# Stores of an attention-score kernel issued in turn by SyncE and ScalarE

## The chip, the cores and the metric

The kernel runs on one core of a Trainium2 chip. The metric is the time of one execution on the device, in microseconds (us), the median over several runs. Below, TensorE is PE, VectorE is DVE, ScalarE is ACT, GpSimd is POOL and SyncE is SP, as the profile names them. The DMA engines are a sixth party: the profile counts 16 of them for the core, and their queues moved 83.89 MB between HBM and the on-chip buffer SBUF. A "ring" here is what the profile lists as the DMA queue of one issuing engine. SyncE's is q1, which holds all 83.89 MB of the kernel before. ScalarE's is q10. A descriptor is one DMA record of the trace: 5120 of the 5504 in q1 before are of 16 KB, the other 384 of 4 bytes. The trace has 16 landings for each transfer, 384 for the 24 transfers; a transfer counts as landed with the last of its 16.

## The reference

For each of 8 x 8 pairs of batch and head, the product of queries and transposed keys, scaled:

```python
def setup_inputs():
    batch, heads, seq, dim = 8, 8, 512, 64
    ...   # q and k, float32, random
def reference(q, k):
    scale = 1.0 / np.sqrt(q.shape[-1])
    return (np.einsum('bhqd,bhkd->bhqk', q, k) * scale).astype(np.float32)
```

The inputs are 16.8 MB and the output 67.1 MB, so writing is four fifths of the traffic.

## The kernel before

The work is cut into four units of two batches. Each has four output tiles of 4 MB (`o`: 128 partitions of 32 KB). All loads and all output tiles share one pool, `big`, of three buffers. Loads are cast by GpSimd, transposed on TensorE, multiplied, and the results are evicted (copied from PSUM, where TensorE writes, to the output tile in SBUF) by ScalarE and VectorE in turn, eight evictions for a tile. When the eighth is done, the tile is stored by one DMA of SyncE.

```python
    big_pool = ctx.enter_context(tc.tile_pool(name="big", bufs=3))
    ...
    def evacuate(dst, src):
        nonlocal n_evac
        if n_evac % 2 == 0:
            pinned(nc.scalar.mul(out=dst, in_=src, mul=scale))
        else:
            pinned(nc.vector.tensor_scalar(out=dst, in0=src, scalar1=scale, ...))
        n_evac += 1
    ...
    def load_and_cast(v):
        xf = big_pool.tile([P, 2, 2, J * D], f32, name="big")
        ...
            nc.sync.dma_start(out=xf[:, x], in_=src[v].rearrange("p (s c) -> p s c", s=2))
        ...
    def scores(v, t):
        kT, qz = ts[v]
        o = big_pool.tile([P, 2, RO, S], f32, name="big")
        for x in range(2):
            for i in range(0, RO, 2):
                ...   # two matmuls into ps
                evacuate(o[:, x, i:i + 2, :], ps)
                yield
        nc.sync.dma_start(out=out_r[v, t], in_=o.rearrange("p x i k -> p x (i k)"))
    ...
    cast = [load_and_cast(v) for v in range(UNITS)]
    ...
    for v in range(UNITS):
        ahead = transpose(v + 1, *cast[v + 1]) if v + 1 < UNITS else iter(())
        for t in range(TILES):
            for n, _ in enumerate(scores(v, t)):
                take(ahead, 1 if v == 0 else int(n in (0, 2, 3, 5, 6)))
```

`pinned` keeps an instruction at its place in the order of its engine.

## Time and profile before

| | before |
|---|---|
| time, median of 3 runs | 202.59 us (202.53 to 202.62) |
| span of the profiled run | 200.7 us |
| VectorE, TensorE, ScalarE busy | 53%, 52%, 42% |
| DMA packets, share of 16 engines | 98.3% in one queue |
| rate over the span | 418 GB/s |

The share of busy time tells which party has no room: here only the DMA engines, at 98.3%. A wait in another engine's row then tells what that engine is held up by. It isn't in itself a cost: after the change the evictions wait 25.5 us longer for TensorE, and the time is the same. The prediction below shows the lines and reads them.

### The profile page before, as it was taken

To read this page: it belongs to the slowest core of one execution; us is meant where nothing else is said; L and a number is where in the kernel's file an instruction comes from. 1 tells how busy PE (TensorE), PEld (TensorE's weight loads), DVE (VectorE), ACT (ScalarE), POOL (GpSimd) and SP (SyncE) were. 2 spreads that over 40 slices of the span, in tenths; PEclk is the share of its full clock that TensorE was granted. 3 is DMA by queue.
4 is the path that set the end of the run, shared out by engine and by line. 5 is a ranking of instruction groups with operands and counts; after the bars stand their busy time and mean duration, and the time that the engine had idled before them with its cause. 6 is when DMAs were issued, how large, how long until landed. Compare 5 with 4: busy or idle time off the path is not lost.

```text
span 200.7 us, 1143 instructions
## 1 busy us (share of the span) xinstructions
PE 105.3 (52%) x384; PEld 45.8 (23%) x384; DVE 106.8 (53%) x98; ACT 85.0 (42%) x97; POOL 39.5 (20%) x22
## 2 busy tenths in 40 slices
PE   0035758566657465478637496748585667510000
PEld 0034535223214131224313122312121111100000
DVE  6705538486475976485749357844444444630000
ACT  2004423864755629253844384366435243620000
POOL 1299999995000000000000000000000000000000
PEclk9999576999699999957999759975858858975555
DMA  6999999999999999999999999999999999999994
GB/s 206 424 444 437 421 421 441 434 395 421 434 424 441 428 431 431 433 426 434 431 428 424 434 441 424 431 431 434 424 431 434 431 424 431 428 437 428 428 428 199
DMA packets 5509, 83.95 MB, mean 418 GB/s; under 512 B 384, under 2 KB 384, under 8 KB 384
## 3 DMA queue, kind: packets, MB, share of 16 engines
q1 hardware_dynamic: 5504, 83.89, 98.3%
q8 instruction: 3, 0.05, 0.1%
q14 instruction: 2, 0.02, 0.0%
HBM read 16.78 MB, written 67.11 MB: 418 GB/s over the span
## 4 chain that ended last, share of the span: by engine, by line
DMA 40%; DVE 10%; PE 8%; ACT 6%; issue 1%; ACTq 0%; SPq 0%; DVEq 0%
DMA out_dram<-big 40%; DVE big L68 9%; PE ps L141 8%; ACT big L66 5%; ACT qz L103 1%; DVE qz L103 1%; ACTq L66 0%; SPq L146 0%; DVEq L68 0%
## 5 line engine op out<-in xcount | busy, mean ns | idle before, releaser
L141 PE MATMUL ps<-kT,qz 128*128 128x512 bf16 x256 | 87.6, 447 | 55.5 <-ACT big L66 41.6
L68 DVE TENSOR_SCALAR big<-ps 128x1024 f32<-128x1024 f32 x64 | 78.4, 1224 | 59.8 <-PE ps L141 37.2
L66 ACT ACTIVATE big<-ps 128x1024 f32<-128x1024 f32 x64 | 65.5, 1023 | 73.0 <-PE ps L141 37.2
L141 PEld LDWEIGHTS <-qz 128*128 128x128 bf16 x256 | 27.2, 106 | 111.0 <-issue 97.5
L89 POOL CAST xb<-big 128x2048 bf16<-128x2048 f32 x16 | 38.8, 2468 | 7.9 <-DMA big<-in_k_dram 7.3
L117 PE MATMUL tp<-identity,xb 128*128 128x128 f32 x64 | 11.6, 346 | 13.4 <-POOL xb L89 13.4
L103 ACT COPY kT<-tp 64x512 f32<-64x512 f32 x16 | 9.2, 577 | 15.3 <-PE tp L117 15.1
L103 DVE COPY kT<-tp 64x512 f32<-64x512 f32 x16 | 11.0, 686 | 6.3 <-PE tp L117 6.0
L117 PEld LDWEIGHTS tp<-identity,xb 128*128 128x128 f32 x64 | 10.5, 184 | 15.2 <-POOL xb L89 13.4
L103 DVE COPY qz<-tp 64x512 f32<-64x512 f32 x16 | 11.0, 687 | 2.7 <-PE tp L125 2.5
L103 ACT COPY qz<-tp 64x512 f32<-64x512 f32 x16 | 9.6, 602 | 2.9 <-PE tp L125 2.7
L125 PE MATMUL tp<-identity,xb 128*128 128x128 f32 x64 | 9.4, 300 | 2.5 <-ACT kT L103 2.5
L125 PEld LDWEIGHTS tp<-identity,xb 128*128 128x128 f32 x64 | 8.5, 156 | 4.3 <-issue 3.3
L156 DVE MEMSET qz<- 128x4096 uint32 x2 | 6.9, 3472 | 2.5 <-PEq L184 1.7
L103 ACT ACT_TABLE_LOAD x1 | 1.3, 1283 | 0.7 <-PEq L184 0.7
masks.py:199 POOL TENSOR_SCALAR_AFFINE_SELECT identity<-identity 128x128 f32<-128x128 f32 x1 | 0.3, 292 | 0.1
masks.py:197 POOL MEMSET identity<- 128x128 f32 x1 | 0.2, 204 | 0.3 <-POOLq L184 0.3
L184 POOL MEMSET const-float32-0.0<- 128x1 f32 x1 | 0.1, 98 | 0.2 <-issue 0.2
L184 POOL MEMSET const-bfloat16-1.0<- 128x1 bf16 x1 | 0.1, 101 | 0.0
L184 POOL MEMSET const-uint8-127<- 128x1 uint8 x1 | 0.1, 101 | 0.0
L184 POOL MEMSET const-float32-1.0<- 128x1 f32 x1 | 0.1, 98 | 0.0
## 6 DMA issues: line engine op xcount, KB each, us to landing
out_dram<-big SPq DMA_DIRECT2D x16, 4096.0 KB, 20.7
big<-in_k_dram SPq DMA_DIRECT2D x4, 2048.0 KB, 18.1
big<-in_q_dram SPq DMA_DIRECT2D x4, 2048.0 KB, 22.7
```

The lines of the kernel that those rows point to most:

```text
L66: pinned(nc.scalar.mul(out=dst, in_=src, mul=scale))
L68: pinned(nc.vector.tensor_scalar(out=dst, in0=src, scalar1=scale, scalar2=None, op0=mybir.AluOpType.mult))
L89: pinned(nc.gpsimd.tensor_copy(out=xb[:, :, s].rearrange("p (g i) d e -> p g e i d", i=wide), in_=xf[:, x, s].rearrange("p (g e i d) -> p ...
L103: pinned(copy(out=dst(s, h), in_=src[:, h]))
L117: pinned(nc.tensor.transpose(out=tp[:, j, :], identity=identity, in_=kb[:, j0 + j]))
L125: pinned(nc.tensor.transpose(out=tp[:, i, jj, :], identity=identity, in_=qb[:, RO * jj + i0 + i]))
L141: pinned(nc.tensor.matmul(out=ps[:, w, :], lhsT=qz[:, i + w, n, :], rhs=kT[:, n].rearrange("d m s j -> d (m s j)"), start=True, stop=True))
L156: nc.vector.memset(qz, 0.0)
L184: nc = _bacc.Bacc("TRN2", target_bir_lowering=False, num_devices=1)
```

## The change

The intent is to let two rings hold queued stores, so that stores can come from two issuers.

```diff
-        nc.sync.dma_start(out=out_r[v, t], in_=o.rearrange("p x i k -> p x (i k)"))
+        queue = (nc.sync, nc.scalar)[t % 2]
+        pinned(queue.dma_start(out=out_r[v, t], in_=o.rearrange("p x i k -> p x (i k)")))
```

## The prediction

The "0 to 0.3 us" for uneven interleaving was the author's guess. So was it that the slowest DMA engine is one that carries the fetch, since the records carry no engine. "That time" is SyncE's time to issue a store, 0.37 us; what follows it is from the trace of before. That the heads of two rings share the engines was an assumption when it was written; how far they do is measured below (96% of the steps change the ring in the run with halves, 27% in the changed kernel).

> **What bounds the kernel now.** I read the page of the profile first, from the top, because the change concerns transfers only and the first question is whether transfers bind.
>
> ```profile
> span 200.7 us, 1143 instructions
> PE 105.3 (52%) x384; PEld 45.8 (23%) x384; DVE 106.8 (53%) x98; ACT 85.0 (42%) x97; POOL 39.5 (20%) x22
> ...
> DMA  6999999999999999999999999999999999999994
> GB/s 206 424 444 437 421 421 441 434 395 421 434 424 441 428 431 431 433 426 434 431 428 424 434 441 424 431 431 434 424 431 434 431 424 431 428 437 428 428 428 199
> ...
> q1 hardware_dynamic: 5504, 83.89, 98.3%
> ...
> HBM read 16.78 MB, written 67.11 MB: 418 GB/s over the span
> ```
>
> No compute engine is busy more than 53%. The row of DMA digits is 9 from the second slice to the last but one, and one queue alone kept the 16 DMA engines occupied for 98.3% of the span. A queue that always has a descriptor ready cannot be made readier by a second queue. I then asked whether these engines are really moving at their pace or only being held by waits. The table by stretch says the first:
>
> ```profile
> core 0: us, PE busy (x) PEld busy (x) DVE busy (x) ACT busy (x) POOL busy (x), PEclk, DMA share, GB/s
> ...
> 92.00:121.00 29.00, 19.13 (x77) 8.29 (x77) 17.18 (x16) 16.78 (x20) 0.00 (x0) 0.87 1.00 429
> 121.00:150.00 29.00, 19.40 (x60) 6.39 (x59) 17.53 (x17) 14.57 (x16) 0.00 (x0) 0.77 1.01 432
> 150.00:178.00 28.00, 16.46 (x46) 4.86 (x44) 14.68 (x12) 12.28 (x12) 0.00 (x0) 0.80 1.01 430
> 178.00:190.00 12.00, 0.00 (x0) 0.00 (x0) 0.02 (x1) 0.00 (x0) 0.00 (x0) 0.50 1.00 427
> ```
>
> The rate is 427 to 432 GB/s with compute beside it and without it (the last row, where all engines but the DMA are done). In the trace's single DMA records the transfer is 5120 descriptors of 16 KB; in every 10 us between 50 and 190 us the median of one is 0.611 us, that is 16384 / 0.611 = 26.8 GB/s for one engine and 429 for 16.
>
> Third, the waits, to see which way round the dependence goes:
>
> ```profile
> ACT big L66 <- DMA out_dram<-big: 31.3, 12, 3.5
> DVE big L68 <- DMA out_dram<-big: 15.5, 9, 2.5
> ```
>
> The evictions wait for stores to land, because the pool "big" has three buffers of 4 MB. Compute is throttled by the stores, not the reverse. Last, the queue's own view and the issue table:
>
> ```profile
> SPq L146 <- DVE big L68: 152.5, 16, 17.6
> ```
>
> ```profile
> out_dram<-big SPq DMA_DIRECT2D x16, 4096.0 KB, 20.7
> ```
>
> SyncE does wait 152.5 us for evictions, and the intent of the change may have come from a line like this. It costs nothing: a store takes 20.7 us from issue to landing while successive stores land some 9.74 us apart ((199.92 - 53.87) / 15, from the landings of the first and the last store in the trace). So about two stores are always with the engines: one moving, one queued behind it in the same ring. What the change wants to create exists already.
>
> [...] Here that time is 0.37 us for a store, 16 x 0.37 = 6 us on an otherwise empty SyncE, never in the way. [...] at 48.42 us a 16 KB instruction fetch of another queue gets in between the stores' descriptors of one engine. It also shows a price: the fetch took 0.961 us and the store's descriptor after it 0.975, both some 0.36 above 0.611. [...]
>
> **The change part by part.**
> - Bytes: unchanged, 83.89 MB, 320 descriptors of 16 KB for each DMA engine. 320 x 0.611 = 195.5 us. The first data starts at 1.75 us; the sum is 197.3. The slowest DMA engine also carries the fetch (0.96 + 0.36 = 1.3 us), which makes 198.6, and some of the turn from loads to stores near 40.5 us, where descriptors took up to 1.24 us; the last data in the trace ends at 199.5, the last landing is at 199.9. None of these terms is removed.
> - SyncE loses 8 issues, worth 8 x 0.37 = 3.0 us of a queue that idles. Gain 0.
> - ScalarE gains 8 issues. The order of instructions shows each placed after ScalarE's last eviction of a tile, waiting for VectorE's last one. At the final tile ScalarE's eviction ended at 176.98 and the store was issued at 178.09, so ScalarE would stand 1.1 us and then, if it costs there what it costs on SyncE, 0.37 us: 1.5 us, 8 times, 12 us on an engine with 85 of 200.7 us busy and 31.3 us of waits for stores before its evictions. Most falls into that wait.
> - What moves: the overlap of stores. Let W = 9.74 us be a store alone and F = 8.4 us the time to fill a tile once its buffer is free (issue minus the landing three stores earlier, or the issue before if later; 7.3 to 9.1 us over the stores from 64 us on). In one ring, when a store's data ends, two whole ones remain, 2W = 19.5 us of work. The landing is noticed about 1.6 us later (my choice: the slowest engine's lag of 1.5 us plus a little), the fill takes 8.4, so 10.0 us later, at the next issue, 9.5 us of work remain. Check: 9.5 + 9.74 + 1.5 = 20.7, the measured issue-to-landing. In two rings the two heads share the engines. When a store ends, the one behind it in its ring is whole and the one in the other ring is half done, so 1.5 W = 14.6 us remain, and at the next issue 4.6 us. The lead halves but stays positive: the DMA would run dry only if a fill took 8.4 + 4.6 = 13.0 us, against 9.1 as the longest. Adding the whole 0.4 us of the issue on ScalarE to F still leaves 4.2.
> - The residence of a store does not change: three buffers turn once in 3W = 29.2 us, of which F = 8.4 is filling, so 20.8 remain for issue to landing.
> - The start: loads keep SyncE's ring and are through at 43.0 us; the first ScalarE store would come at about 47.5 us, so no load is delayed. The end: the last two stores share the engines and finish with the total work, as before.
>
> Sum: 0 removed from the path, 0 to 0.3 us added by uneven interleaving. The time is 202.59 + 0.1 = 202.7 us (the span plus the same 1.9 us as now).
>
> **The rivals.**
> - Changing rings has a price. If each of the 256 store descriptors of a DMA engine lost the 0.36 us seen beside the fetch, 92 us would be added; a loss of 0.016 us each already makes 4 us, 2%. For it: the two lengthened descriptors. Against it: [...] the turn from loads to stores in one ring lengthened descriptors likewise, so I take the direction, not the ring, as the cause. Here both rings only write. I give it 8%, mostly as a small loss: 204 to 215 us.
> - The rings run dry. Stores that land together would free two buffers at once and leave one store with 9.7 us of work against a fill of 8.4. That is tight, and each tile that needs more than 9.7 would lose the difference, perhaps 0.5 us. Against it: one stream of compute fills tiles one after another, which puts the stagger back. 1 us in all, 203.6 us.
> - Two rings hide gaps between descriptors or stores. The table of stretches shows a DMA share of 1.00 to 1.01, so there are no gaps to hide[...].
> - A lucky placement of the fetch or of the slow engine: up to 1.3 us gained, 201.3 us.
>
> **Range and chances.** 201.4 to 204.8 us: below, the slow engine's lag gone; above, a ring dry now and then or a switch that costs 0.008 us. Faster by over 2% would need 198.5 us, less than the 198.6 of the sum above: 0.02. Slower by over 2% (206.7 us) is the price of switching: 0.07. Within 2%: 0.91.
>
> **What would show it.** Two hardware queue rows in place of one, with ScalarE's about 33.6 MB and a total share near 98%; 427 to 432 GB/s in every stretch after 64 us; a median issue-to-landing near 20.8 us on both queues; eight issues on ScalarE of some 0.4 us; evictions still waiting for stores, in total much as now. Descriptors of more than 0.63 us in the median would prove me wrong on switching, slices of DMA below 9 in the middle on dry rings[...].

## The result, and the profile after

The changed kernel takes 202.53 us (median of 4 runs, 202.52 to 202.61). The kernel before took 202.56 us in the same rounds (4 runs). The ratio is 1.0001, with a 95% interval of 0.9983 to 1.0018. A ratio here and below is the mean time of one kernel's runs over that of the other's runs of the same rounds, so it isn't quite the ratio of the medians quoted. Executions over 1.5% slower than the fastest of the same kernel are left out of the means.

From the page of the changed kernel: first span and busy shares, then the DMA share and rate in 40 slices, then queues with packets, MB and share of 16 engines.

```profile
span 200.7 us, 1129 instructions
PE 108.2 (54%) x384; PEld 47.1 (23%) x384; DVE 106.8 (53%) x98; ACT 85.0 (42%) x97; POOL 39.5 (20%) x22
...
DMA  6999999999999999999999999999999999999994
...
q1 hardware_dynamic: 3328, 50.33, 59.3%
q10 hardware_dynamic: 2176, 33.55, 39.1%
```

The DMA digits are the same 40 characters as before. The two queues together hold the DMA engines for 59.3 + 39.1 = 98.4% of the span, where one held them for 98.3%. Half of the written bytes did move to ScalarE's queue, and nothing was gained by it because there was no idle time to fill (a DMA share of 1.00 to 1.01 in the stretches before).

The same stretches as shown of before (time, busy time of each engine with counts, granted clock, DMA share, GB/s):

```profile
92.00:121.00 29.00, 19.15 (x72) 7.99 (x72) 18.23 (x19) 16.22 (x20) 0.00 (x0) 0.82 1.00 428
121.00:150.00 29.00, 17.25 (x60) 6.76 (x60) 16.82 (x16) 13.99 (x16) 0.00 (x0) 0.79 1.01 431
150.00:178.00 28.00, 17.77 (x47) 5.30 (x46) 13.47 (x11) 12.01 (x12) 0.00 (x0) 0.74 1.00 427
178.00:190.00 12.00, 4.05 (x9) 0.87 (x7) 3.67 (x3) 2.31 (x3) 0.00 (x0) 0.64 1.02 434
```

The rate is 427 to 434 GB/s, before 427 to 432. In the last row compute still runs, where before it had ended: the last store was issued at 184.0 us and not at 178.1. Its last data still landed at 199.92 us, the very same time as before. So compute got 6 us later without any cost.

The waits of engines (engine and line, waited for, total us, times, longest us); in the issue table below, the last column is the median us from issue to landing:

```profile
DVE big L68 <- PE ps L141: 51.8, 46, 4.7
ACT big L66 <- PE ps L141: 48.1, 46, 3.8
...
ACT big L66 <- DMA out_dram<-big: 19.4, 6, 4.6
...
ACT big L66 <- DVE big L68: 5.2, 3, 2.2
...
DVE big L68 <- DMA out_dram<-big: 5.0, 2, 3.4
```

Before, the first two of these were:

```profile
DVE big L68 <- PE ps L141: 37.2, 40, 1.8
ACT big L66 <- PE ps L141: 37.2, 41, 3.4
```

SyncE's own wait, and the issue table:

```profile
SPq L147 <- DVE big L68: 149.5, 8, 21.7
```

```profile
out_dram<-big SPq DMA_DIRECT2D x8, 4096.0 KB, 19.3
out_dram<-big ACTq DMA_DIRECT2D x8, 4096.0 KB, 18.0
```

Three things moved. The evictions' waits for stores fell from 31.3 + 15.5 = 46.8 us to 24.4 us. Their waits for TensorE grew from 74.4 to 99.9 us, so most of the idle time only changed its name. And ScalarE has a new wait of 5.2 us for VectorE: it stands at its DMA instruction until VectorE's last eviction is done, at one store from 64.95 us until VectorE ends at 66.64, with the issue at 66.72.

I worked some more numbers out of the single DMA records of the traces, in which each descriptor has a start and a duration. The work left at an issue is the number of descriptors issued and not yet ended, times 0.611 us, over 16 engines. The fill is counted as in the prediction. The lag is the last of a transfer's 16 landings minus their median; the median stands for the end of the store's data.

| from the fifth store on (fill and next store: from the fourth) | before | after |
|---|---|---|
| work left in the rings at an issue | 8.8 to 10.9 us | 4.0 to 7.4 us |
| work left of the next store when a store's data ends | 9.7 to 10.0 us | 6.6 to 9.7 us, mean 8.3 |
| fill of a tile, mean | 8.2 us | 8.9 us (longest 10.6) |
| median duration of a 16 KB descriptor | 0.611 us | 0.611 us |
| lag of the slowest DMA engine, apart from the last store | 1.3 to 1.7 us | 2.4 to 3.3 us |

The lead of the queue nearly halved (mean 9.9 to 5.7 us), as forecast, and was never used up. The last row I had not forecast.

### The profile page after: what moved, and what is told of

Same layout as the page of the kernel before. It is cut to its first block, busy times and chain, and to the rows that moved or that the text cites. A ratio compares the mean times of both kernels' runs of the same rounds, so it can differ in the third digit from the quotient of the medians.

```text
span 200.7 us, 1129 instructions
## 1 busy us (share of the span) xinstructions
PE 108.2 (54%) x384; PEld 47.1 (23%) x384; DVE 106.8 (53%) x98; ACT 85.0 (42%) x97; POOL 39.5 (20%) x22
## 3 DMA queue, kind: packets, MB, share of 16 engines
q1 hardware_dynamic: 3328, 50.33, 59.3%
q10 hardware_dynamic: 2176, 33.55, 39.1%
## 4 chain that ended last, share of the span: by engine, by line
DMA 30%; PE 16%; DVE 14%; ACT 7%; issue 1%; DVEq 0%; SPq 0%; ACTq 0%
DMA out_dram<-big 30%; PE ps L141 15%; DVE big L68 14%; ACT big L66 6%; ACT qz L103 1%; PE tp L117 1%; DVEq L68 0%; SPq L147 0%; ACTq L66 0%
## 5 line engine op out<-in xcount | busy, mean ns | idle before, releaser
L141 PE MATMUL ps<-kT,qz 128*128 128x512 bf16 x256 | 89.6, 465 | 58.4 <-DVE big L68 31.5
L141 PEld LDWEIGHTS <-qz 128*128 128x128 bf16 x256 | 28.0, 110 | 115.4 <-issue 102.5
L117 PE MATMUL tp<-identity,xb 128*128 128x128 f32 x64 | 10.8, 329 | 13.6 <-POOL xb L89 13.6
L103 ACT COPY kT<-tp 64x512 f32<-64x512 f32 x16 | 9.2, 577 | 15.5 <-PE tp L117 15.3
L125 PE MATMUL tp<-identity,xb 128*128 128x128 f32 x64 | 10.7, 329 | 2.5 <-ACT kT L103 2.5
## 6 DMA issues: line engine op xcount, KB each, us to landing
out_dram<-big SPq DMA_DIRECT2D x8, 4096.0 KB, 19.3
```

Source lines behind the costliest of these rows:

```text
L103: pinned(copy(out=dst(s, h), in_=src[:, h]))
L117: pinned(nc.tensor.transpose(out=tp[:, j, :], identity=identity, in_=kb[:, j0 + j]))
L125: pinned(nc.tensor.transpose(out=tp[:, i, jj, :], identity=identity, in_=qb[:, RO * jj + i0 + i]))
L141: pinned(nc.tensor.matmul(out=ps[:, w, :], lhsT=qz[:, i + w, n, :], rhs=kT[:, n].rearrange("d m s j -> d (m s j)"), start=True, stop=True))
```

## The experiments

Theory: the DMA engines set the pace with 83.9 MB at 0.611 us for 16 KB, and the number of rings and the issuing engine only change the order. The rivals were: (A) two rings did gain something and ScalarE's new work took it back, (B) changes of ring have a price, (C) a second ring hides the start of stores, (D) the halved lead costs something.

Twelve kernels ran. "Half" kernels are wrong. All seven others gave correct results.

### One ring, all stores from ScalarE

```diff
-        queue = (nc.sync, nc.scalar)[t % 2]
+        queue = nc.scalar
```

> All 16 stores are issued by ScalarE, so there is one ring again, but ScalarE carries 16 issues of 0.38 us and the waits for VectorE ahead of them. Theory (the DMA engines set the pace, and the issuing engine does not matter): 202.6 us, within 0.5 us of the kernel before; the work left in the ring at an issue is near 9.9 us as before and not near 5.5 us as after, and the slowest DMA engine lands about 1.5 us behind the median one. Rival A (two rings gave something that the cost on ScalarE took back): the cost is now doubled and the gain gone, so slower than before by the cost of 16 issues, 6 us or more, 208 us. Rival B (changing rings has a small price): a little faster than after.

Measured: 202.75 us (4 runs), the kernel before 202.48 in the same rounds, ratio 1.0009 (0.9994 to 1.0024). Sixteen issues on ScalarE in place of none moved the median by 0.3 us, so rival A, which asked for 6 us or more, falls. The lag was 1.0 to 1.8 us, that of one ring. The work left at an issue was not near 9.9 us all along. It was 2.7 to 5.3 us from 59 to 96 us and grew to about 10 us by 140 us. The third store was issued at 59.4 us, before at 56.6, and the lead had to build up again.

### Each store in two halves, one for each ring

```diff
-        queue = (nc.sync, nc.scalar)[t % 2]
-        pinned(queue.dma_start(out=out_r[v, t], in_=o.rearrange(...)))
+        rows = o.rearrange("p x i k -> p x (i k)")
+        for x, queue in enumerate((nc.sync, nc.scalar)):
+            pinned(queue.dma_start(out=out_r[v, t][:, x], in_=rows[:, x]))
```

> Every store is cut in two halves of 2 MB, one for each ring, issued together. Both rings then always work on the same tile, so that tiles land one after another as in one ring, while the DMA engines change rings all the time. Theory: 202.6 us, within 0.5 us of before; descriptors stay at 0.611 us in the median though the rings now alternate for nearly all of the stores; tiles are about 20 us from issue to landing; the slowest DMA engine's lag is back at about 1.5 us, where it was 3.1 us with stores of different tiles in the two rings. Rival B (a change of rings costs time, but in the changed kernel the rings overlapped too little to show it): with 256 changes for each DMA engine even 0.02 us each adds 5 us, 207 us.

Measured: 203.42 us (4 runs), ratio 1.0040 (1.0025 to 1.0055). My 0.5 us was missed: this is 0.9 us slower, and clear of noise. The design also wasn't what I had written. SyncE issues the first half as soon as that head is evicted, 4 to 5 us before the other half. The records do show the two rings alternating descriptor by descriptor for most of the run. When they are joined into one sequence for each engine, as described under the late loads below, 96% of the steps from one descriptor to the next between 92 and 121 us change the ring. In the changed kernel only 27% do (64 to 180 us), so that kernel alone says little about the price of a change. The median stayed at 0.611 us, so the 5 us of rival B didn't come. The lag was up to 3.3 us, not 1.5. The stretch from 92 to 121 us:

```profile
92.00:121.00 29.00, 19.04 (x73) 7.86 (x72) 18.33 (x18) 15.94 (x20) 0.00 (x0) 0.85 1.01 431
```

With rings changing all the time, 431 GB/s, within the 427 to 432 of the kernel before.

### Halves in the last three quarters only

```diff
+        if v == 0:
+            pinned(nc.sync.dma_start(out=out_r[v, t], in_=rows))
+        else:
+            for x, queue in enumerate((nc.sync, nc.scalar)):
+                ...
```

> Halves in both rings again, but only for the stores of the last three quarters; the first four stores go whole through SyncE as in the kernel before. The run with all halves was 0.9 us slower than the kernel before, although its descriptors kept 0.611 us. If those 0.9 us came from the start, where the first halves interleave with the last loads at 38 to 41 us and 38 descriptors were lengthened instead of 27: 202.3 to 202.8 us, as before. If they came from the changes of ring all along, three quarters of them stay: 203.1 us or more.

Measured: 203.15 us (5 runs), the kernel before 202.54, ratio 1.0028 (1.0016 to 1.0041). By the expectation's own rule the start is not the main cause, and that guess of mine fell. What the records show is a spread of small parts: the last data ended at 199.72 us, before at 199.49; the last landing came 0.66 us later still, before 0.43; and the program ended 1.1 us after that, before 0.8. Descriptors had a mean of 0.616 us in both. Which mechanism makes these 0.6 us stays open. They bound the price of a ring change all the same: if the whole 0.6 us came from the up to 192 descriptors of one DMA engine in the halved stores, each would cost 0.003 us.

### Two buffers in place of three, one ring and two

```diff
-    big_pool = ctx.enter_context(tc.tile_pool(name="big", bufs=3))
+    big_pool = ctx.enter_context(tc.tile_pool(name="big", bufs=2))
```

> The kernel before with two buffers of 4 MB in place of three, so that the lead of the ring at an issue, 9.9 us with three buffers, goes to nearly nothing. It is the partner of the next run. Estimate: a fill of 8.4 us starts at a landing, which comes 1.5 us after the median data end, and an issue on an empty ring takes about 1 us to the first data, so each pair of stores leaves the DMA engines dry for 1 to 2 us, and the first store is some 6 us later because it needs the buffer of the third load: 212 to 226 us. If it stays near 203 us, the buffers were not what the evictions waited for, and my reading of the waits is wrong.

> The changed kernel with two buffers. Theory (the second ring only changes the order in which queued stores move): with a thin lead there is hardly a queued store for it to reorder, so within 2% of the run with two buffers and one ring. Rival C (a second ring hides the start of a store behind the end of the one before, and three buffers had hidden it already): faster than its partner by up to 1 us a store, 14 us in all, 6%. Rival D (the rings share evenly from the moment of issue, so that the lead is halved here too): slower than its partner, by some 10 us.

Measured: 217.13 us with one ring (4 runs, ratio to before 1.0714) and 219.25 us with two (4 runs, 1.0829), so two rings over one is 1.0829 / 1.0714 = 1.011. The DMA rows of the pages, one ring first:

```profile
DMA  6999999629899989999989994999899999979996
```

```profile
DMA  6999999639599999998989996999997999979996
```

Now there are slices below 9, and the time grew: the evictions' waits for stores now reach the DMA engines, which three buffers had prevented. With one ring the engines idle 5.9 us between 36 and 50 us, where the first store comes 10 us later than before, and 8.3 us after that. Here, if anywhere, a second ring could have filled gaps. It did not: rival C would have been up to 6% faster. Nor did it cost the 10 us of rival D. The 2 us that it did cost are idle time after 50 us (10.6 in place of 8.3 us); ScalarE's pauses could make them, but no run tests that. These runs also bear on why sharing is weaker than I had thought. With the DMA engines empty, a store's first descriptor started 0.9 us after its issue. In the changed kernel, with the other ring busy, that took 2.3 to 4.3 us, so where little work is left at an issue (0 to 3.4 us with two buffers and one ring), stores in two rings hardly overlap, by my estimate. Why the start is late, no run shows.

### Half the bytes: the first head of each tile

The issuing engine is left out of the diff.

```diff
-  dma_start(out=out_r[v, t], in_=o.rearrange("p x i k -> p x (i k)"))
+  dma_start(out=out_r[v, t][:, 0:1], in_=o.rearrange("p x i k -> p x (i k)")[:, 0:1])
```

> The kernel before, but each store writes only the first half of its tile (a wrong result on purpose: half of the output is never written). The DMA engines have 50.3 MB instead of 83.9, 117 us of work. Theory: compute becomes the bound: the first store at 36.8 us, then 15 tiles at 8.4 us, then 5 us for the last half store and 3 us for landing and the rest, about 172 us, with the DMA idle between stores. If the time stays above 195 us, transfers were not the bound. It is the partner of the next run.

> The changed kernel with the same half stores (wrong result on purpose). Nothing hides ScalarE's part of the change here. Theory: each of the 8 issues on ScalarE costs the path between 0.4 us (the issue alone) and 1.5 us (with the wait for VectorE's last eviction), so 3 to 12 us more than the run with half stores and one ring, my guess 5 us, 3%: the change then has a price that the full stores hid. Rival: ScalarE's pause is absorbed because it waits for TensorE at a tile's start anyway, and the two runs agree within 1 us. Second rival: with two rings the half stores land sooner and it is faster.

Measured: 165.19 us with one ring and 171.60 with two (4 runs each, of which one each slow; ratios to before 0.8127 and 0.8468). With transfers cut, the time fell by 37 us, so transfers were the bound; my 172 us for one ring was 7 us too long. The pair differs by 6 to 7 us, but I couldn't credit that to ScalarE's pause: the first head is ready in the middle of a tile, where SyncE issues it at once (4 to 5 us before the other half in the run with halves), while ScalarE reaches its instruction only at the tile's end. So the next three runs repeat it with a better half.

### Half the bytes: the last four rows of both heads, three issuers

Again without the issuing engine:

```diff
-  dma_start(out=out_r[v, t], in_=o.rearrange("p x i k -> p x (i k)"))
+  dma_start(out=out_r[v, t][:, :, S * RO // 2:],
+            in_=o.rearrange("p x i k -> p x (i k)")[:, :, S * RO // 2:])
```

One kernel has SyncE alone, one `(nc.sync, nc.scalar)[t % 2]`, one `(nc.sync, nc.gpsimd)[t % 2]`.

> A better pair than the half stores of before. There each store wrote the first head of a tile, so SyncE could issue it in the middle of the tile and ScalarE only at its end, and the last store came later for that reason alone. Now each store writes the last four of eight rows of both heads (half the bytes again, wrong result on purpose), so it depends on the last eviction of the tile, as the full store does. One ring, all by SyncE: compute is the bound, about 168 us, that is the 165 us of the first half stores plus the last store now issued some 3 us later.

> The same half stores, issued in turn by SyncE and ScalarE. Theory (ScalarE's pause before and during its issue, up to 1.5 us each, is on the path as soon as the DMA engines are not the bound): 3 to 10 us more than its partner, my guess 5 us. Rival (most of the 6 us between the first pair came from where in the tile the store was issued): less than 2 us more.

> The same half stores in turn from SyncE and GpSimd: two queues again, but the second issuer has nothing else to do after its casts end at about 48 us. If ScalarE's pause is what costs, this is within 1 us of the run with one ring (166 to 170 us). If two queues as such cost, it is as slow as the run with ScalarE.

Measured, 4 runs each: 169.51 us for SyncE alone (ratio to before 0.8381), 175.83 us with ScalarE (0.8668), 168.84 us with GpSimd (0.8354). With ScalarE it is 175.83 - 169.51 = 6.3 us longer, by the ratios 0.8668 / 0.8381 = 1.034, and a second issuer that is otherwise idle costs nothing. Two queues as such are not the cost. One rival remains for a part of the 6.3 us: the granted TensorE clock was 0.86 to 0.91 in the runs with ScalarE and 0.90 to 0.95 in those with SyncE alone. The SyncE run at 0.904 took 171.12 us, the three ScalarE runs at 0.907 to 0.913 took 174.22 to 175.86. So at a like clock 3 to 5 us stay with ScalarE's part. The DMA row with SyncE alone shows how far transfers are from binding:

```profile
DMA  6999999999949476556838591919192939293856
```

With ScalarE, its waits gain a line that the run with SyncE alone does not have, and one stretch of the timeline (start, duration, instruction, idle before it and what ended that) shows one such pause:

```profile
ACT big L66 <- DVE big L68: 9.4, 5, 2.2
```

```profile
113.89 0.58 ACT L103 COPY kT<-tp 64x512 f32<-64x512 f32 x1
...
114.32 1.23 DVE L68 TENSOR_SCALAR big<-ps 128x1024 f32<-128x1024 f32 x1 [1.10 <-PE ps L141]
...
115.63 0.38 ACTq L147 DMA_DIRECT2D out_dram<-big  x1
...
116.11 1.02 ACT L66 ACTIVATE big<-ps 128x1024 f32<-128x1024 f32 x1 [1.64 <-DVE big L68]
```

ScalarE ends its copy at 114.47, stands until VectorE's eviction ends at 115.55, issues for 0.38 us, and evicts again at 116.11: 1.64 us of idle time. Over the kernel, 3 to 6 us for eight issues are 0.4 to 0.8 us each, less than such a pause. That the rest lies where ScalarE would have waited anyway is my reading; it was not measured by itself.

### Loads among the stores, in the same ring and in the other

```diff
-    cast = [load_and_cast(v) for v in range(UNITS)]
+    cast = [load_and_cast(v) for v in range(UNITS - 1)]
     ...
         for t in range(TILES):
+            if (v, t) == (1, 0):
+                cast.append(load_and_cast(UNITS - 1))
```

The second of the pair adds, in the load:

```diff
+            queue = nc.scalar if v == UNITS - 1 else nc.sync
```

> The kernel before with the last pair of loads (4 MB) moved from the start to the second quarter, among the stores, in the same ring. Partner of the next run. Expected: descriptors lengthened to 0.7 to 1.2 us at the two turns between loads and stores, some 16 to 32 at each turn as at 40 us in the kernel before, and 0.611 us elsewhere; the time some us above 202.6, because a buffer is taken for load and cast in the middle (205 to 215 us).

> The same late loads, issued by ScalarE, so that loads in one ring and stores in the other alternate on every DMA engine for some 10 to 20 us. It tests the argument of the prediction that the 0.36 us seen beside an instruction fetch came from the change of direction, not of ring. If the direction costs: descriptors alternate and most of the up to 512 in that stretch take 0.7 to 1.0 us, 2 to 6 us of DMA time are lost, and the rate there falls below 400 GB/s. If neither direction nor ring costs anything in a running stream: 0.611 us as elsewhere, and the lengthened descriptors belong to single fetches only. Time within 5 us of its partner.

Measured, one run each of unknown state: 208.37 us in the same ring and 213.46 us in the other. They are 5.1 us apart, where I had expected at most 5. The times only say that the moved load disturbs the buffers. The descriptors are what I looked for. The records carry no engine, but joining each start to the end that it follows gives 16 sequences. In the second run, from 62 to 82 us, most of them read "store, load, store, load" (84% of the steps change the ring). From 63 us on in that stretch, 251 load descriptors have a mean of 0.611 us and 247 store descriptors one of 0.614 us. Where it begins, 15 of the 16 sequences hold one store descriptor of 1.21 us, twice the usual, and most of them one or two of 0.66 to 1.1 us ahead of it. The rate in the middle of the second run:

```profile
64.00:70.00 6.00, 0.00 (x0) 0.00 (x0) 0.00 (x0) 0.00 (x0) 0.00 (x0) 0.50 1.01 431
70.00:76.00 6.00, 2.17 (x5) 0.66 (x5) 2.34 (x3) 2.05 (x2) 2.43 (x2) 0.50 1.00 426
```

So alternating reads and writes in two rings ran at the full 426 to 431 GB/s. Neither the change of ring nor the change of direction costs anything that shows in a running stream; most engines lose some 0.7 to 1.1 us once, when it begins. The run with one ring has such losses too: 31 lengthened descriptors where the loads begin (73 to 77 us) and 40 where the stores come back (83 to 87 us), 0.8 and 1.0 us for each DMA engine. So the loss at a turn needs no change of ring. With two rings the beginning cost 0.9 us and the end of the loads nothing.

## Why the prediction was right, point by point

- **The bound.** Right. The time is the data of the 16 DMA engines: 98.3% busy before, 98.4% after, 0.611 us for a descriptor in both, last landing at 199.92 us in both. Fewer bytes made it faster by 33 to 37 us, thinner buffers slower by 15 us, and the issuing engine did neither.
- **SyncE's 152.5 us of waiting is free.** Right. The line is 149.5 us for 8 stores after, and the time is the same.
- **"ScalarE gains 8 issues": 1.5 us each, 12 us.** Roughly right in size, and right that it is free here. An issue took 0.378 us. The changed kernel has seven pauses (after the eighth issue ScalarE has no work left) of 1.3 to 3.8 us from ScalarE's last work to its next, 15.6 us in all, with whatever waits for TensorE they contain. With full stores they cost nothing. With half stores the kernel was 6.3 us longer, 3 to 5 us at a like clock.
- **The lead halves, 9.5 to 4.6 us.** Right in number (9.9 to 5.7 us in the mean), in part by luck. It measured 8.8 to 10.9 before and 4.0 to 7.4 after. Its terms were off and worked against each other. The landing is noticed not 1.6 but up to 3.3 us late, and the fill took 8.9 and not 8.4 us (8.2 in the kernel before), both of which shrink the lead. But "the one in the other ring is half done" was wrong. A store starts only 2.3 to 4.3 us after its issue, so stores share less than I had assumed, and the next one has 8.3 us left in the mean when one ends, not the 4.9 us of half a store.
- **"The residence of a store does not change", 20.8 us.** Too long: the table's medians are 19.3 and 18.0 us. The mis-sized term is the cycle of three buffers: with longer fills a freed buffer sometimes waits for the tile before it to be finished (one store landed at 105.09 us, and the tile then in work was issued at 106.74 us), and that time is lacking in the residence.
- **Evictions would wait for stores "in total much as now".** Wrong: 46.8 us became 24.4. Part of that slack went into longer fills: 13 fills are longer by 8.9 - 8.2 = 0.7 us each, 9 us. The other side of the account is the evictions' waits for TensorE, which grew by 25.5 us. It had no effect on the time since none of it was on the path.
- **The first rival: "so I take the direction, not the ring, as the cause" of the lengthened descriptors.** The conclusion, no price for changing rings, was right, but this argument for it was wrong. Direction alternating descriptor by descriptor cost nothing either (0.611 us for loads, 0.614 for stores, with 84% of the steps changing the ring). What the 0.36 us beside an instruction fetch comes from, no run here settles. The trace does not show where the fetch reads. The text names one place of this kind; in the trace of before there are three (48.42, 98.92 and 157.41 us), each with a fetch of 0.95 to 0.96 us and a store descriptor of 0.98 to 0.99 us after it.
- **The second rival, dry rings.** Did not happen with three buffers. The least lead was 3.0 us, at the second store. With two buffers there was hardly a lead to halve (0 to 3.4 us at an issue with one ring).
- **The third, gaps to hide.** None: the rate stayed at 427 to 434 GB/s.

No version here beats both kernels. 320 descriptors of 0.611 us make 195.5 us on each DMA engine, and the bytes are fixed by the shapes of float32 inputs and outputs.

## What to carry to other kernels

Before adding a second queue, look whether the first one ever runs empty: here the DMA engines were busy in every slice but the first and the last (98.3% of the span) and stores waited behind stores, and another ring added nothing (202.53 against 202.56 us). Even where it did run empty, with two buffers, the second ring didn't help (219.25 against 217.13 us), because the stores themselves came late. An engine that computes paid for a DMA with more than the issue, since it stood in order until the last writer of the tile was done: 1.64 us of idle time around an issue of 0.38 us. That was free while transfers were the bound, and some 0.4 to 0.8 us a store as soon as they were not, so give stores to an engine that is otherwise idle (with half stores 168.84 us with GpSimd as the second issuer, 175.83 with ScalarE).
